# An encoder layer on one core: query transposes taken two heads at a time, the low parts of queries and keys later in VectorE's order, four weight casts later in the read-out

## The chip, the cores and the metric

The kernel runs on one core of a Trainium2 chip. The metric is the device time of one execution in microseconds (us). Before the change it is 1470.08 us, the median of three runs (1469.82 to 1471.71). The profile shows one further execution.

The engines are called by the profile's names: PE (TensorE matmul), PEld (its weight loads), DVE (VectorE), ACT (ScalarE), POOL (GpSimd) and SP, whose queue issues most DMAs.

## The reference, cut to what matters

One layer of a bidirectional encoder is applied to two sequences of 512 tokens with 1024 features. A state-space branch and a windowed attention branch are computed from the same normalized rows, gated, added, projected, and followed by a squared-ReLU MLP. The change touches the normalized queries and keys of the attention branch, and the place at which the key weights are prepared.

```
q, k, v, u, g_att, g_ssm = jnp.split(h @ w_in, IN_SPLITS, axis=-1)
q = rms_norm(q.reshape(bsz, seq_len, N_HEADS, HEAD_DIM), q_gain)     # 16 heads of 64
k = rms_norm(k.reshape(bsz, seq_len, N_KV_HEADS, HEAD_DIM), k_gain)  # 4 heads of 64
...
s = jnp.einsum('nqkgd,njkd->nkgqj', qb, kw) * scale + bias   # blocks of 128, three neighbours
s = jnp.where(mask[:, None, None], s, NEG_INF)
p = jax.nn.softmax(jnp.concatenate([s, sink_col], axis=-1), axis=-1)[..., :-1]
o = jnp.einsum('nkgqj,njkd->nqkgd', p, vw)
```

## The kernel before, in words

**Split numbers.** Products are made of float32 values split in a high part (rounded to fp32r, written by ACT) and a low part (the rest, written by DVE). A score product takes queries whose 128 rows hold the high part of 64 features in one half and the low part in the other, and keys that hold the same 64 features in both halves. So one product with the keys' high part `kh` and one with their low part `kl` give the whole score, whichever half of the queries is the high one.

**Read-out stage** (lines 890 to 950, about 326 to 414 us of the profile). A loop over 32 pairs of state groups, `q` in `range(NQ)`: the tables of pair q+5 are ordered on SP, `read_out(q)` multiplies on PE, `gelu(q)` takes the result out of PSUM on ACT. Beside it the stage works off a list of other products, and the table `casts` says behind which pair a quarter of the key weights `w_k` (and later of the value weights `w_v`) is loaded, cast to its high part by ACT, and given a low part by DVE. The staging tile of such a load (`c_raw`, `w_raw`) has two buffers. PE, ACT and DVE follow the written order here; SP's order is the scheduler's.

**Attention stage** (the function entered at line 1120, loop at 1199; about 451 to 685 us). A step is a pair (key head j, sequence sq), eight in all; a step has four units, one for each block of 128 queries (`qb` 0 to 3), and all of PE, ACT, DVE and POOL follow the written order. The document calls units by `qb`: a unit with qb 0 or 3 has scores 256 wide, one with qb 1 or 2 has 384. In each unit stand, interleaved:

- the scores and minima of the current unit (`cur.scores(h)`, `cur.largest(h)`, `cur.exp(h)` for four heads h). `largest` is one DVE instruction, L1052, that reads the score bank; there are two such banks, so `scores(2)` waits for `largest(0)`, and the next unit's `scores(0)` for `largest(2)`.
- the values of the unit before (`prev`): for each of its two or three key blocks i, four transposes on PE (`turn(i)`, L1064), a high part on ACT (`high(i)`, `ph`), a low part on DVE (`low(i)`, `pl`, L1073), and two products on PE (`value(i, 0)` with `ph`, `value(i, 1)` with `pl`, both L1080). `prev` has three blocks in the units qb 2 and 3, two in qb 0 and 1. Behind them ACT copies the lower half of the sums (`ol`, L1084), which DVE adds one unit later (`owed.add()`, L1090).
- a tile of the next step's queries: `project` on PE (L724), `square` on ACT and `power` on DVE and POOL, `norm` on DVE (L1012); then, one unit later and under the name `rows`, four transposes (`rows.turn()`, L1018), `rows.high()` on ACT (L1023) and `rows.low()` on DVE (L1027). Before the transposes POOL copies each head's 64 features a second time beside the first (L1013), so that a transpose of one head gives them in both halves.
- in a unit qb 0, the next step's keys: `key_copies` on POOL, `key_turn` (PE L981, ACT L982 for `kh`, DVE L983 for `kl`).
- in the units qb 1 and 2 of most steps, the low part of a piece of the next query weights (`lower`, `w_lo`, L719).

PSUM: scores have two banks, the transposes `tps` two, `acc` (projections and turned queries) three, and the sums `po` one.

Before the loop, `entry()` handles the first four query tiles and the values; tiles 0 to 2 are turned there, tile 3 in the loop's first unit.

Of the kernel before, what the change touches and what calls it, by code (L numbers as in the profile page):

```python
# [18 lines left out]
P = 128  # L19
# [44 lines left out]
def hybrid_layer(ctx, tc, x, xT, rel, onehot, early, w_qkv, w_ug, q_gain, k_gain, sink,  # L64
# [707 lines left out]
    with tc.tile_pool(name="ssmo", bufs=2, reuse_waits="tile") as sp:  # L772
# [129 lines left out]
        def last_cast():  # L902
            cast_owed.pop(0)()
            return dve_owed.pop()

        casts = {0: [last_cast], 1: [last_cast], 2: [lambda: w_k.piece(0)], 3: [lambda: w_k.piece(1)], 8: [lambda: w_k.piece(2)], 9: [lambda: w_k.piece(3)],
                 17: [lambda: w_v.piece(0)], 18: [lambda: w_v.piece(1)], 20: [lambda: w_v.piece(2)], 21: [lambda: w_v.piece(3)]}
# [45 lines left out]
    with tc.tile_pool(name="att", bufs=2, reuse_waits="tile") as ap:  # L953
# [21 lines left out]
        def key_turn(j, sq, kd):  # L975
            kh = ap.tile([P, HALF], F32R, tag="kh", name="kh")
            kl = ap.tile([P, HALF], F32R, tag="kl", name="kl")
            keys[j, sq] = (kh, kl)
            ps = tps()
            for t in range(4):  # L980
                PE.transpose(ps[:, t * P:(t + 1) * P], kd[:, t].rearrange("p a d -> p (a d)"), ident)  # L981
            S.activation(kh, ps, AF.Copy, scale=gain_k)  # L982
            V.scalar_tensor_tensor(kl, ps, gain_k, kh.bitcast(F32), op0=ALU.mult, op1=ALU.subtract)  # L983
            queries[j, sq] = ap.tile([P, G, HALF], F32R, tag="qa", name="qa")

        class Tile:
# [23 lines left out]
            def norm(self):  # L1010
                self.qn = ap.tile([P, G, 2, HD], F32, tag="qn", name="qn")
                V.tensor_mul(self.qn[:, :, 0], self.psv, self.rq[:, :, None].to_broadcast([P, G, HD]))  # L1012
                GP.tensor_copy(self.qn[:, :, 1], self.qn[:, :, 0])  # L1013

            def turn(self):
                self.pt = acc()
                for h in range(G):
                    PE.transpose(self.pt[:, h * P:(h + 1) * P], self.qn[:, h].rearrange("p a d -> p (a d)"), ident)  # L1018

            def high(self):  # L1020
                self.ptv = self.pt.rearrange("p (h t) -> p h t", h=G)
                self.dst = queries[self.key][:, :, self.t * P:(self.t + 1) * P]
                S.activation(self.dst, self.ptv, AF.Copy, scale=gain_q)  # L1023

            def low(self):
                dst = self.dst[64:128]
                V.scalar_tensor_tensor(dst, self.ptv[64:128], gain_q[64:128], dst.bitcast(F32),  # L1027
                                       op0=ALU.mult, op1=ALU.subtract)

# [100 lines left out]
        def entry():  # L1130
# [6 lines left out]
            for t in range(4):  # L1137
# [3 lines left out]
                if t == 0:  # L1141
                    key_turn(0, 0, kd)
                if old:
# [48 lines left out]
        pending = []  # L1192
        prev = owed = lower = None
        y_rows, made = [], None
# [4 lines left out]
        if True:  # L1199
            rows = entry()  # L1200
            for i, (j, sq) in enumerate(steps):
# [8 lines left out]
                for qb in range(NB):  # L1210
# [12 lines left out]
                    cur.scores(0)  # L1223
                    cur.largest(0)
                    if rows and not rows.qn:
                        rows.power()
# [3 lines left out]
                    if owed:  # L1230
                        owed.add()
                    cur.largest(1)
                    if n3:
                        prev.turn(0)
# [45 lines left out]
                    if kd:  # L1280
                        key_turn(*nxt, kd)
                    if div:
# [9 lines left out]
                    if rows:  # L1292
                        if not sooner:
                            rows.high()
                        rows.low()
                    project(4)
# [24 lines left out]
                if i == len(steps) - 2:  # L1321
                    hpool_cm.__exit__(None, None, None)
                    slot_a, slot_b = [opers.enter_context(tc.tile_pool(name=f"slot_{n}", bufs=1, side="right", reuse_waits="tile"))
                                      for n in "ab"]
                    y_tiles = [[[t_[:, 0:4, :], t_[:, 4:8, :]] for t_ in slot(slot_a)], split_slot()]
            ahead = Column(1)
            gs0 = wyp.tile([P, T, NSEQ, NCHUNK], F32, tag="y_lo", name="gs")
# [732 lines left out]
```

## Time and profile before

| | us |
|---|---|
| median of three runs | 1470.08 |
| profiled execution, its device time | 1469.22 |
| its span from first to last instruction | 1467.4 |
| entry and attention stage, about | 424 to 685 |
| read-out stage, about | 326 to 414 |

The profile page gives busy time and share of the span of each engine, the chain of work that ended last, and groups of instructions by line, engine and operation, with the idle time ahead of them and what ended it. The timeline lists instructions in order of time: start, duration, engine, line, operation, tiles written and read, and in brackets the idle time of that engine ahead of it with what released it. A row with x2 or x4 merges as many equal instructions. The profile's 1467.4 us lie 1.8 us below the execution's own time, and that lies 0.9 us below the median.

### The profile page before, as it was taken

How to read it: one execution, taken by the hardware profiler on the slowest of the kernel's cores; microseconds unless marked ns; L12 is line 12 of the kernel's file. 1: busy time of each engine (PE TensorE's matmuls, PEld its weight loads, DVE VectorE, ACT ScalarE, POOL GpSimd, SP SyncE). 2: the span in 40 equal slices, each digit the busy share in tenths (PEclk: the TensorE clock that was granted, in tenths of full speed). 3: DMA queues.
4: the chain of work that ended last, by engine and by line, in shares of the span. 5: the costliest groups of instructions: out<-in, count | busy, mean ns of one | idle time of the engine just before them, and what ended most of it. 6: DMA issues, size and time to landing. Idle time of an engine off the chain costs nothing.

```text
span 1467.4 us, 21580 instructions
## 1 busy us (share of the span) xinstructions
PE 1446.3 (99%) x7782; PEld 1234.1 (84%) x7782; DVE 1094.6 (75%) x1836; ACT 764.2 (52%) x1366; POOL 168.9 (12%) x270
## 2 busy tenths in 40 slices
PE   6999999999999999999999999999999999999998
PEld 5888888888999899987888888888888888888887
DVE  7799979975636889888974689877776588575653
ACT  5489862233426778787532355554554444333332
POOL 4111120000223333343101000000000000000000
PEclk9999999999999999999999999999999999999999
DMA  8355567259941413236964134544443894454441
GB/s 300 112 171 174 161 206 268 101 178 290 307 131 35 121 46 89 95 130 217 303 212 144 72 115 165 174 149 147 155 158 123 302 346 147 158 177 153 129 129 58
DMA packets 129239, 243.86 MB, mean 166 GB/s; under 512 B 16060, under 2 KB 59324, under 8 KB 129133
## 3 DMA queue, kind: packets, MB, share of 16 engines
q1 hardware_dynamic: 104684, 186.87, 40.4%
q10 hardware_dynamic: 21888, 46.15, 8.3%
q0 software_dynamic: 2560, 9.48, 2.0%
q8 instruction: 61, 1.00, 0.3%
q14 instruction: 46, 0.37, 0.1%
HBM read 173.20 MB, written 81.82 MB: 174 GB/s over the span
## 4 chain that ended last, share of the span: by engine, by line
PE 91%; DVE 3%; ACT 2%; DMA 1%; issue 1%; POOL 1%; SPq 0%; DVEq 0%; ACTq 0%; POOLq 0%
PE bank L115 14%; PE bank L116 14%; PE bank L117 14%; PE acc L141 11%; PE acc L724 8%; PE acc L753 5%; PE acc L115 3%; PE acc L117 3%; PE acc L116 3%; PE po L1080 2%; PE sps L604 2%; PE sps L1048 2%; PE sps L860 2%; PE tps L1064 2%; PE lag L619 1%
## 5 line engine op out<-in xcount | busy, mean ns | idle before, releaser
L116 PE MATMUL bank<-b_lo,a_hi 128*128 128x512 f32 x440 | 171.2, 389 | 0.0
L117 PE MATMUL bank<-b_hi,a_lo 128*128 128x512 f32 x440 | 171.2, 389 | 0.0
L115 PE MATMUL bank<-b_hi,a_hi 128*128 128x512 f32 x440 | 171.2, 389 | 0.0
L724 PE MATMUL acc<-w_hi,hT 128*128 128x256 f32 x768 | 165.0, 291 | 0.0
L141 PE MATMUL acc<-hT,c_hi 128*128 128x512 f32 x512 | 161.1, 394 | 0.0
L1933 ACT CAST a_hi<-d_a 128x1024 fp32r<-128x1024 f32 x55 | 58.0, 1054 | 178.1 <-PE bank L116 175.2
L1934 DVE TENSOR_TENSOR a_lo<-d_a,a_hi 128x1024 fp32r<-128x1024 f32 x55 | 67.3, 1223 | 99.4 <-ACT a_hi L1933 97.3
L724 PEld LDWEIGHTS acc<-w_hi,hT 128*128 128x128 f32 x768 | 126.7, 190 | 1.7
L141 PEld LDWEIGHTS acc<-hT,c_hi 128*128 128x128 f32 x512 | 94.6, 188 | 21.0 <-issue 2.5
L724 PE MATMUL acc<-w_lo,hT 128*128 128x256 f32 x384 | 108.2, 282 | 0.0
L141 PE MATMUL acc<-hT,c_lo 128*128 128x512 f32 x256 | 100.3, 392 | 0.0
L115 PE MATMUL bank<-act,u_hi 128*128 128x512 f32 x256 | 99.6, 389 | 0.0
L116 PE MATMUL bank<-act,u_hi 128*128 128x512 f32 x256 | 99.6, 389 | 0.0
L117 PE MATMUL bank<-act,u_lo 128*128 128x512 f32 x256 | 99.6, 389 | 0.0
L117 PEld LDWEIGHTS bank<-b_hi,a_lo 128*128 128x128 f32 x440 | 82.6, 188 | 17.3
L115 PEld LDWEIGHTS bank<-b_hi,a_hi 128*128 128x128 f32 x440 | 82.6, 188 | 17.1
L116 PEld LDWEIGHTS bank<-b_lo,a_hi 128*128 128x128 f32 x440 | 82.6, 188 | 17.1
L1058 ACT ACTIVATE p<-p,nmx 128x257 f32<-128x257 f32 (+1 forms) x128 | 72.1, 564 | 27.0 <-DVE nmx L1052 24.3
L724 PEld LDWEIGHTS acc<-w_lo,hT 128*128 128x128 f32 x384 | 73.0, 190 | 2.5
L1052 DVE CUSTOM_DVE_ANT_0 p<-sps,bias,nsink 128x256 f32<-128x256 f32 (+1 forms) x128 | 69.2, 541 | 2.9 <-PE sps L1048 0.4
L1717 ACT CAST u_hi<-s 128x512 fp32r<-128x512 f32 x64 | 39.3, 621 | 59.8 <-PE bank L116 43.1
L1934 DVE TENSOR_TENSOR b_lo<-k,b_hi 128x1024 fp32r<-128x1024 f32 x55 | 66.9, 1217 | 0.0
(387 smaller groups left out, 3622.9 us busy)
## 6 DMA issues: line engine op xcount, KB each, us to landing
d_a<-a_scr SPq DMA_DIRECT2D x55, 512.0 KB, 3.6
u_raw<-in_w_up_dram SPq DMA_DIRECT2D x32, 512.0 KB, 5.7
a_scr<-t ACTq DMA_DIRECT2D x64, 256.0 KB, 2.1
k<-in_w_down_dram SPq DMA_DIRECT2D x32, 512.0 KB, 5.7
a_scr<-a ACTq DMA_DIRECT2D x48, 256.0 KB, 3.3
c_raw<-in_w_ug_dram SPq DMA_DIRECT2D x44, 256.0 KB, 3.6
ct_scr<-ctab SPq DMA_DIRECT2D x16, 576.0 KB, 3.3
ctab_in<-ct_scr SPq DMA_DIRECT2D x32, 288.0 KB, 4.7
```

The costliest lines, as they stand in the source:

```text
L115: PE.matmul(ps, a[0], b[0], start=first, stop=False)
L116: PE.matmul(ps, a[0], b[1], start=False, stop=False)
L117: PE.matmul(ps, a[1], b[0], start=False, stop=last)
L141: PE.matmul(self.ps[s], self.w[p == 2][:, k, :], hT[s][p == 1][:, k, :], start=i % (3 * KT) == 0, stop=i % (3 * KT) == 3 * KT - 1)
L604: PE.matmul(ps[:, i * P:(i + 1) * P], bm[:, ri, g, :], u_sb[:, g, :], start=True, stop=True)
L724: PE.matmul(ps, act[p == 2][:, k, col:col + P], self.w[k // 4][p == 1][:, k % 4, :], start=i == 0, stop=i == 3 * KT - 1)
L753: PE.matmul(self.ps[s], w_g[self.m][p == 2][:, k, :], y_part(s, int(p == 1), k), start=k + p == 0, stop=k == KT - 1 and p == 2)
L1052: V.tensor_tensor_reduce(self.p[:, h, 1:1 + self.nk], self.s[h][:, 0:self.nk], biases[self.j][h][:, b0:b0 + self.nk], -1.0, nsink[:, hh:hh ...
L1058: S.activation(p, p, AF.Exp, bias=self.nmx[:, h:h + 1], scale=-1.0, accum_out=self.sums[:, h, self.qb:self.qb + 1])
L1717: S.copy(hi, src)
L1933: S.copy(hi, src)
L1934: V.tensor_sub(lo, src, hi.bitcast(F32))
```

## The change

Four things change.

1. **Queries.** `norm` writes each head once, without POOL's copy. `turn` transposes two heads at a time, so two transposes in place of four; the first head of a pair comes out in rows 0 to 63, the second in rows 64 to 127. `high` becomes two ACT instructions on 64 rows, one for the first heads and one for the second, each with 2x128 elements in a row in place of one with 4x128 on 128 rows; `low` becomes two DVE instructions of that shape, each writing the half of the rows that its input does not lie in.
2. **Place of the queries' low part.** In the loop it is held back (`low_rows`) and written in the next unit, behind `largest(1)`.
3. **Place of the keys' low part.** `key_turn` returns it; in the loop it is held back (`low_keys`) and written in the next unit (qb 1) behind `largest(0)`. In `entry()` it follows at once, as before.
4. **Casts of the key weights.** The quarters stand behind the pairs 4, 6, 9 and 11 in place of 2, 3, 8 and 9.

```diff
-        casts = {0: [last_cast], 1: [last_cast], 2: [lambda: w_k.piece(0)], 3: [lambda: w_k.piece(1)], 8: [lambda: w_k.piece(2)], 9: [lambda: w_k.piece(3)],
+        casts = {0: [last_cast], 1: [last_cast], 4: [lambda: w_k.piece(0)], 6: [lambda: w_k.piece(1)], 9: [lambda: w_k.piece(2)], 11: [lambda: w_k.piece(3)],
...
-            V.scalar_tensor_tensor(kl, ps, gain_k, kh.bitcast(F32), op0=ALU.mult, op1=ALU.subtract)
             queries[j, sq] = ap.tile([P, G, HALF], F32R, tag="qa", name="qa")
+            return lambda: V.scalar_tensor_tensor(kl, ps, gain_k, kh.bitcast(F32), op0=ALU.mult, op1=ALU.subtract)
...
             def norm(self):
-                self.qn = ap.tile([P, G, 2, HD], F32, tag="qn", name="qn")
-                V.tensor_mul(self.qn[:, :, 0], self.psv, self.rq[:, :, None].to_broadcast([P, G, HD]))
-                GP.tensor_copy(self.qn[:, :, 1], self.qn[:, :, 0])
+                self.qn = ap.tile([P, G, HD], F32, tag="qn", name="qn")
+                V.tensor_mul(self.qn, self.psv, self.rq[:, :, None].to_broadcast([P, G, HD]))
...
             def turn(self):
                 self.pt = acc()
-                for h in range(G):
-                    PE.transpose(self.pt[:, h * P:(h + 1) * P], self.qn[:, h].rearrange("p a d -> p (a d)"), ident)
+                for m in range(G // 2):
+                    PE.transpose(self.pt[:, m * P:(m + 1) * P], self.qn[:, 2 * m:2 * m + 2].rearrange("p a d -> p (a d)"), ident)
...
             def high(self):
-                self.ptv = self.pt.rearrange("p (h t) -> p h t", h=G)
-                self.dst = queries[self.key][:, :, self.t * P:(self.t + 1) * P]
-                S.activation(self.dst, self.ptv, AF.Copy, scale=gain_q)
+                q = queries[self.key][:, :, self.t * P:(self.t + 1) * P].rearrange("p (m e) t -> p m e t", e=2)
+                pt = self.pt[:, 0:G // 2 * P].rearrange("p (m t) -> p m t", m=G // 2)
+                self.halves = []
+                for e, (own, other) in enumerate(((slice(0, 64), slice(64, P)), (slice(64, P), slice(0, 64)))):
+                    hi, lo, src = q[own, :, e], q[other, :, e], pt[own]
+                    S.activation(hi, src, AF.Copy, scale=gain_q[own])
+                    self.halves.append((hi, lo, src, gain_q[own]))
...
             def low(self):
-                dst = self.dst[64:128]
-                V.scalar_tensor_tensor(dst, self.ptv[64:128], gain_q[64:128], dst.bitcast(F32),
-                                       op0=ALU.mult, op1=ALU.subtract)
+                for hi, lo, src, gain in self.halves:
+                    V.scalar_tensor_tensor(lo, src, gain, hi.bitcast(F32), op0=ALU.mult, op1=ALU.subtract)
...
                     cur.largest(0)
+                    if low_keys:
+                        low_keys()
+                        low_keys = None
...
                     cur.largest(1)
+                    if low_rows:
+                        low_rows()
+                        low_rows = None
...
                     if kd:
-                        key_turn(*nxt, kd)
+                        low_keys = key_turn(*nxt, kd)
...
                         if not sooner:
                             rows.high()
-                        rows.low()
+                        low_rows = rows.low
```

The lines of the changed kernel stand some three lines further down, so L1052 of before is L1055 there, L1027 is L1031, L1073 is L1076.

The first place is DVE's order around the start of a unit qb 1 (here of the second step). Before, from the keys' low part at the end of the unit qb 0 to the first `pl`:

```order
L983 SCALAR_TENSOR_TENSOR kl<-tps,gain_k,kh 128x512
L1027 SCALAR_TENSOR_TENSOR qa<-acc,gain_q,qa 64x4x128
L1052 ISA p,nmx<-sps,bias,nsink 128x384
L1052 ISA nmx 128x1
L1005 TENSOR_REDUCE ms<-sq 128x4
L1090 TENSOR_TENSOR ya<-po,ol 64x2x128 x2
L1052 ISA p,nmx<-sps,bias,nsink 128x384
L1052 ISA nmx 128x1
L1073 TENSOR_TENSOR pl<-tps,ph 128x512
```

The same place of the changed kernel, from the unit's first minimum to its first `pl`:

```order
L1055 ISA p,nmx<-sps,bias,nsink 128x384
L1055 ISA nmx 128x1
L984 SCALAR_TENSOR_TENSOR kl<-tps,gain_k,kh 128x512
L1005 TENSOR_REDUCE ms<-sq 128x4
L1093 TENSOR_TENSOR ya<-po,ol 64x2x128 x2
L1055 ISA p,nmx<-sps,bias,nsink 128x384
L1055 ISA nmx 128x1
L1031 SCALAR_TENSOR_TENSOR qa<-acc,gain_q,qa 64x2x128 x2
L1076 TENSOR_TENSOR pl<-tps,ph 128x512
```

Both low parts stood ahead of the first minimum; now both stand between the first minimum and the first `pl`. In the other units the queries' low part moves in the same way, and there is no `kl`.

The second place is ACT's order in the read-out, behind the last cast of the gates (`c_hi`). `ysb` is a pair's `gelu`, `st` the turning of a later pair's states. Before:

```order
L868 ACTIVATE ysb<-sps 128x256
L872 DMA y_scr<-ysb 128x512
L718 CAST w_hi<-w_raw 128x512
L868 ACTIVATE ysb<-sps 128x256
L845 COPY st<-h 64x512
L718 CAST w_hi<-w_raw 128x512
```

After:

```order
L868 ACTIVATE ysb<-sps 128x256
L872 DMA y_scr<-ysb 128x512
L868 ACTIVATE ysb<-sps 128x256
L845 COPY st<-h 64x512
L151 COPY sg<-acc 128x8x64
L868 ACTIVATE ysb<-sps 128x256
L872 DMA y_scr<-ysb 128x512
L718 CAST w_hi<-w_raw 128x512
```

The first cast stands two `gelu` later. On SP the load of its data keeps its place; the third and fourth loads of `w_raw` stand two sets of tables further back than before.

More of the change, by code (lines that the diff above doesn't have):

```diff
@@ L1141, in entry @@
                 if t == 0:
-                    key_turn(0, 0, kd)
+                    key_turn(0, 0, kd)()
                 if old:
@@ L1192, in hybrid_layer @@
         pending = []
-        prev = owed = lower = None
+        prev = owed = lower = low_rows = low_keys = None
         y_rows, made = [], None
@@ L1325, in hybrid_layer @@
                     y_tiles = [[[t_[:, 0:4, :], t_[:, 4:8, :]] for t_ in slot(slot_a)], split_slot()]
+            assert not low_rows and not low_keys
             ahead = Column(1)
```

## The prediction

> **What bounds the kernel now.** The page comes first: who is busy, and through whom the chain that ended last runs.
>
> ```profile
> PE 1446.3 (99%) x7782; PEld 1234.1 (84%) x7782; DVE 1094.6 (75%) x1836; ACT 764.2 (52%) x1366; POOL 168.9 (12%) x270
> ...
> PE 91%; DVE 3%; ACT 2%; DMA 1%; issue 1%; POOL 1%; SPq 0%; DVEq 0%; ACTq 0%; POOLq 0%
> ```
>
> PE carries the kernel, so a PE instruction less should shorten it. But the change lies in the attention stage, and there the second engine counts too. The windows of one step (one unit in a row, qb 0 to 3, each from its first score product to the next unit's):
>
> ```profile
> core 0: us, PE busy (x) PEld busy (x) DVE busy (x) ACT busy (x) POOL busy (x), PEclk, DMA share, GB/s
> 538.22:544.69 6.47, 6.47 (x53) 6.29 (x52) 4.98 (x16) 4.44 (x12) 2.36 (x5) 1.00 0.01 3
> 544.69:552.05 7.36, 7.32 (x51) 6.44 (x50) 6.93 (x19) 6.15 (x17) 1.80 (x4) 1.00 0.01 3
> 552.05:559.46 7.41, 7.41 (x57) 7.04 (x56) 6.83 (x17) 6.55 (x17) 1.84 (x4) 1.00 0.45 133
> 559.46:566.60 7.14, 7.14 (x56) 6.72 (x55) 6.17 (x17) 5.79 (x16) 4.16 (x6) 1.00 0.56 164
> ```
>
> The clock is full, PE has no slack, but DVE is at 92 to 94% in the middle units. So I ask when DVE's results are due. PE multiplies `pl` i in `value(i, 1)`, and stands still if `pl` is late. DVE's timeline of that step:
>
> ```profile
> 538.66 0.48 DVE L1052 CUSTOM_DVE_ANT_0 p<-sps,bias,nsink 128x256 f32<-128x256 f32 x1
> ...
> 540.68 0.69 DVE L1073 TENSOR_TENSOR pl<-tps,ph 128x512 fp32r<-128x512 f32 x1
> ...
> 544.45 0.75 DVE L983 SCALAR_TENSOR_TENSOR kl<-tps,gain_k,kh 128x512 fp32r<-128x512 f32 x1 [1.35 <-ACT kh L982]
> ...
> 546.31 0.62 DVE L1052 CUSTOM_DVE_ANT_0 p<-sps,bias,nsink 128x384 f32<-128x384 f32 x1
> ...
> 547.18 0.84 DVE L1090 TENSOR_TENSOR ya<-po,ol 64x256 f32<-64x256 f32 x2
> ...
> 548.60 0.69 DVE L1073 TENSOR_TENSOR pl<-tps,ph 128x512 fp32r<-128x512 f32 x1
> ...
> 550.14 0.68 DVE L719 TENSOR_TENSOR w_lo<-w_raw,w_hi 128x512 fp32r<-128x512 f32 x1
> 550.75 0.68 DVE L1073 TENSOR_TENSOR pl<-tps,ph 128x512 fp32r<-128x512 f32 x1
> ...
> 551.88 0.08 DVE L1052 DVE_READ_ACCUMULATOR2_ANT nmx<- 128x1 f32 x1
> 551.99 0.76 DVE L1027 SCALAR_TENSOR_TENSOR qa<-acc,gain_q,qa 64x512 fp32r<-64x512 f32 x1
> 552.78 0.62 DVE L1052 CUSTOM_DVE_ANT_0 p<-sps,bias,nsink 128x384 f32<-128x384 f32 x1
> ...
> 558.27 0.68 DVE L1073 TENSOR_TENSOR pl<-tps,ph 128x512 fp32r<-128x512 f32 x1
> ...
> 560.50 0.49 DVE L1052 CUSTOM_DVE_ANT_0 p<-sps,bias,nsink 128x256 f32<-128x256 f32 x1
> ...
> 562.52 0.69 DVE L1073 TENSOR_TENSOR pl<-tps,ph 128x512 fp32r<-128x512 f32 x1
> ```
>
> And PE's products that read these `pl`, with the transposes L1018 and a score product:
>
> ```profile
> 541.95 0.40 PE L1080 MATMUL po<-pl,va 128*128 128x512 f32 x1
> ...
> 544.88 0.34 PE L1048 MATMUL sps<-kl,qa 128*128 128x384 f32 x1
> ...
> 549.34 0.51 PE L1080 MATMUL po<-pl,va 128*128 128x512 f32 x1
> ...
> 551.50 0.47 PE L1080 MATMUL po<-pl,va 128*128 128x512 f32 x1
> ...
> 557.37 0.60 PE L1018 MATMUL acc<-ident,qn 128*128 128x128 f32 x4
> ...
> 559.22 0.39 PE L1080 MATMUL po<-pl,va 128*128 128x512 f32 x1
> ...
> 563.26 0.50 PE L1080 MATMUL po<-pl,va 128*128 128x512 f32 x1
> ```
>
> The reader is to see how close they are. `pl` ends at 548.60 + 0.69 = 549.29, PE starts 0.05 later: it waited. It waited at 563.26 too (562.52 + 0.69 + 0.05). At 551.50 the margin is 0.02, at 559.22 it is 0.22, at 541.95 it is 0.53. And DVE starts a unit late where the low parts stand ahead of it: its first minimum is 0.44 after the unit's start in qb 0, but 1.62 in qb 1, 0.73 in qb 2, 1.04 in qb 3.
>
> **The change part by part.**
>
> *Transposes.* L1018's group gives a mean of 277 ns, but four of them take 0.60, so they start (0.60 - 0.277)/3 = 0.108 us apart.
>
> ```profile
> L1018 PE MATMUL acc<-ident,qn 128*128 128x128 f32 x128 | 19.7, 277 | 1.2 <-POOL qn L1013 1.2
> ```
>
> Two fewer save 0.22 in each of 32 tiles, 6.9 us in all, but they stand behind `value(0, 1)`: a wait there is not shortened by them. The Trainium skill ("TensorE: Matmul & The Clock Gate", Part 4: PE-mode transpose) gives some 275 ns for such a transpose in a kernel's context; counted so, 64 of them would be 17.6 us. The row has that duration, but the starts are 0.108 apart, so the measurement decides for 6.9.
>
> *The low part, now a pair, in a new place.* One instruction of 64x256 of this kind is not in the trace. The additions L1090 have its shape: 0.42 each. The kind costs 0.07 more (0.76 against 0.69 at 512 elements), so 0.49, twice 0.98. Ahead of it the trace shows 0.11 (551.88 to 551.99) in place of an immediate start, behind it 0.03 (551.99 + 0.76 to 552.78). Together **1.12 us** between the second minimum and the first `pl`. Bounds: 0.79, if the pair took no longer than the single one with its gap, and 1.3. The Trainium skill ("VectorE: DVE Perf Modes", Two Vector instructions with no wait between them) says that an instruction whose start quadrant differs from the one before is held until that has finished; the pair changes halves each time, so all would be held. The gaps of 0.11 and 0.03 agree; without holding, the overlaps seen elsewhere would make it about 0.8, and the sum below 8 us smaller.
>
> *What moves earlier in return.* DVE no longer has the low part ahead of the first minimum, which then starts 0.04 after its scores (544.88 + 0.34): 0.57 into a 384-wide unit, 0.44 into a 256-wide one. But the additions behind it need ACT's `ol`, made at the start of a unit:
>
> ```profile
> 559.00 0.67 ACT L1023 ACTIVATE qa<-acc,gain_q 128x512 fp32r<-128x512 f32 x1
> 559.58 0.37 ACT L1001 ACTIVATE sq<-acc 128x256 f32<-128x256 f32 x1
> 559.97 0.58 ACT L1084 COPY ol<-po 64x512 f32<-64x512 f32 x1
> ```
>
> `ol` ends 1.09 into the unit. ACT's pair has sq's size, so 0.4 each, 0.8 for 0.58: `ol` comes 0.2 later (0.37 at most, with the 0.08 that the gain costs in the row above). So I credit qb 3 with 0.23 of its 0.60, qb 2 with nothing of its 0.16, and qb 1 with all 1.05, since `kl` gives `ol` time there.
>
> *By unit*, with every later DVE row of a unit moving along:
> - qb 0: `pl` ends 541.37 + 1.12 = 542.49, PE at 542.54 for 541.95: +0.59 - 0.22 = **+0.37**.
> - qb 1: -1.05 + 0.68 (`kl`, its 0.75 less 0.07 of overlap as behind `w_lo`) + 1.12 = 0.75. The second `pl` ends 551.43 + 0.75, PE at 552.23 for 551.50: **+0.73**; the saved transposes lie ahead of that wait.
> - qb 2: the third `pl` ends 558.95 + 1.12, PE at 560.12 for 559.22: **+0.90**.
> - qb 3: the first `pl` is 0.89 later, PE too: +0.89 - 0.22 = **+0.67**.
>
> A step grows by 2.67. Five steps (the second to fifth and the seventh) have this form: 13.4. The sixth has no `w_lo`, so its later `pl` aren't late and only the first is: 2.0 by the same working. In the eighth, without projections, I set nothing (between -1 and +1).
>
> *First step and entry.* Two waits go there: POOL's copy ahead of the transposes, and the first minimum behind `kl`.
>
> ```profile
> 455.60 0.66 PE L1018 MATMUL acc<-ident,qn 128*128 128x128 f32 x4 [0.82 <-POOL qn L1013]
> ...
> 460.11 0.44 PE L1048 MATMUL sps<-kh,qa 128*128 128x384 f32 x1 [0.47 <-DVE nmx L1052]
> ...
> L1013 POOL COPY qn<-qn 128x256 f32<-128x256 f32 x32 | 12.7, 398 | 29.7 <-DVE qn L1012 25.5 <-PE sps L1048 3.6 <-PE tps L1064 0.6
> ```
>
> The copy's 0.40 and 0.22 go in its unit qb 0; qb 1 comes out about even (-0.1), qb 2 and 3 grow by 0.9 and 0.7: +0.9. The entry saves three times 0.22, with PE always busy: -0.7. POOL's other copies lie beside PE's work: nothing.
>
> *Read-out.* ACT stood before the first key cast until its data had landed, and PE behind it, since `gelu` frees its banks:
>
> ```profile
> 336.10 0.62 ACT L718 CAST w_hi<-w_raw 128x512 fp32r<-128x512 f32 x1 [5.70 <-DMA w_raw<-in_w_qkv_dram]
> ...
> 337.06 0.49 PE L858 MATMUL sps<-u_sb,toep 128*128 128x128 f32 x2 [0.61 <-ACT ysb L868]
> 338.31 0.68 PE L860 MATMUL sps<-st,ctab_in 128*128 128x128 f32 x4 [0.77 <-ACT st L845]
> ```
>
> Two pairs later the data lies there, as its DMA keeps its place on SP. 0.61 + 0.77: **-1.4** (0 if another cast or a later load on SP takes over, -1.8 with PE's restarts).
>
> **Sum:** 13.4 + 2.0 + 0.9 - 0.7 - 1.4 = +14.2 on the profiled execution's 1469.2, which lies 0.9 below the median: **1483 us**, slower by 0.9%.
>
> **The rivals.**
>
> *PE keeps the bound.* DVE's busy time in the step is 24.9 of 28.4, four times 0.33 more would fit, and its waits for ACT's halves go:
>
> ```profile
> DVE qa L1027 <- ACT qa L1023: 10.5, 21, 0.8
> ...
> PEld po L1080 <- DVE pl L1073: 2.2, 8, 0.3
> ```
>
> Then 6.9 for the transposes, 1.4 in the read-out, these 2.2, and the first step's 0.4 and 0.5 go: 1469.2 - 11.4 = **1458**. It decides if `pl` still comes before PE asks, which in qb 1 needs both halves in under 0.4 us. The margins above speak against it: it is the place and not the total that counts. By the skill's 275 ns it would be 1447.
>
> *Even.* Each 0.1 less for the pair takes about 2.6 off (26 units). At 0.58 the gains elsewhere cancel the waits: **1469**. No row has two such instructions in that time.
>
> *The halves add their time and no more.* With the lower bound 0.79 the sum is 14.2 - 8.6 = 5.6: **1475**; that lies in the forecast's own case.
>
> **How the numbers follow.** The forecast's case, slower, has 0.72; PE keeping the bound 0.15; even 0.13. What a measurement of this kernel can tell from no change is about 0.2%, 3 us, so these are also the chances of slower, faster and same. The upper end takes 1.3 for the pair (+4.7): 1488. The lower goes past 0.79 for the pair to 1468, which covers the even case and leaves out the PE-bound one.
>
> **What would show it.** Right: in the units qb 0 to 3 PE waits in front of L1080 for `pl`, some 0.6 to 1.1 us a unit in place of 2.2 us over the stage; the units last about 6.8, 8.1, 8.3 and 7.8; the pair's instructions take 0.49; the wait at 337 is gone. Wrong: units shorter by 0.2 with no wait at L1080 (PE's bound), or instructions of the pair well under 0.4. DVE no longer waits for ACT's query halves in either case.

## The result, and the profile after

| | before | after |
|---|---|---|
| median of 4 runs each, us | 1469.95 (1469.59 to 1471.71) | 1488.34 (1487.40 to 1489.23) |
| ratio | | 1.0124, 95% interval 1.0109 to 1.0139 |
| profiled execution: span, us | 1467.4 | 1487.5 |

The change makes the kernel 1.2% slower, 18.4 us; the prediction said 13 (1483), and its range ended at 1488, just below the measured median. Direction and mechanism were right, the size was not.

The page of the changed kernel, busy engines and the chain that ended last:

```profile
PE 1445.8 (97%) x7718; PEld 1228.7 (83%) x7718; DVE 1104.8 (74%) x1868; ACT 774.7 (52%) x1398; POOL 154.6 (10%) x238
...
PE 80%; DVE 10%; ACT 4%; issue 3%; DMA 2%; POOL 1%; SPq 0%; DVEq 0%; ACTq 0%; POOLq 0%
```

PE is busy no longer than before, with 64 instructions less, and the span is 20 us longer: the difference is waiting. DVE, 3% of the chain before, now holds 10%. The view of waits over the attention stage says for what (engine and line, what it waited for and who made it; us in total, times, longest). First the kernel before, then the changed one, both from 451 to 700 us:

```profile
PEld po L1080 <- DVE pl L1073: 3.9, 12, 0.5
...
PE po L1080 <- DVE pl L1073: 0.4, 2, 0.2
```

```profile
PEld po L1083 <- DVE pl L1076: 34.4, 44, 1.4
...
PE po L1083 <- DVE pl L1076: 21.7, 35, 1.1
DVE ya L1093 <- ACT ol L1087: 2.8, 15, 0.2
```

The weight loads' wait for `pl`, 3.9 us before (2.2 in the prediction's row, which leaves out both ends of the stage), is now 34.4; that of the products, 0.4 before, is 21.7. The windows of the units qb 0 to 3 (qb 0 is the first row and belongs to the next step; columns as in the prediction):

```profile
573.27:580.25 6.98, 6.54 (x52) 6.15 (x50) 5.45 (x16) 4.86 (x13) 1.96 (x4) 1.00 0.07 23
548.70:556.82 8.12, 7.05 (x50) 6.20 (x49) 7.33 (x19) 6.65 (x19) 1.41 (x3) 1.00 0.01 3
556.82:565.35 8.53, 7.72 (x55) 6.74 (x54) 7.28 (x18) 6.54 (x17) 2.86 (x3) 1.00 0.40 114
565.35:573.27 7.92, 7.02 (x54) 6.51 (x52) 6.33 (x17) 6.20 (x17) 2.34 (x5) 1.00 0.58 158
sum 31.55, PE 28.32 PEld 25.60 DVE 26.39 ACT 24.26 POOL 8.57; mean PE 7.08 PEld 6.40 DVE 6.60 ACT 6.06 POOL 2.14
```

Units of 6.98, 8.12, 8.53 and 7.92 stand where 6.47, 7.36, 7.41 and 7.14 stood: a step is 3.2 longer, and no engine is full in it. The order of DVE in qb 2 shows why (timeline):

```profile
557.36 0.62 DVE L1055 CUSTOM_DVE_ANT_0 p<-sps,bias,nsink 128x384 f32<-128x384 f32 x1 [0.65 <-PE sps L1051]
...
558.51 0.84 DVE L1093 TENSOR_TENSOR ya<-po,ol 64x256 f32<-64x256 f32 x2 [0.19 <-ACT ol L1087]
559.38 0.62 DVE L1055 CUSTOM_DVE_ANT_0 p<-sps,bias,nsink 128x384 f32<-128x384 f32 x1
559.93 0.08 DVE L1055 DVE_READ_ACCUMULATOR2_ANT nmx<- 128x1 f32 x1
560.04 0.98 DVE L1031 SCALAR_TENSOR_TENSOR qa<-acc,gain_q,qa 64x256 fp32r<-64x256 f32 x2
561.05 0.69 DVE L1076 TENSOR_TENSOR pl<-tps,ph 128x512 fp32r<-128x512 f32 x1
...
564.26 0.69 DVE L1076 TENSOR_TENSOR pl<-tps,ph 128x512 fp32r<-128x512 f32 x1
```

The pair sits where the prediction put it: 0.11 behind the second minimum (559.93 to 560.04), 0.98 long, 0.03 ahead of `pl`. DVE waits at the unit's start, for scores and then for ACT's `ol`, and has the 1.12 us to do after that, so the first `pl`, and with it PE's product, comes later.

Where the 18 us lie, by the first score product of each step in the two profiled executions:

| | predicted | measured |
|---|---|---|
| up to the attention loop (read-out, entry) | -2.1 | -2.3 |
| first step | +0.9 | +1.3 |
| steps 2 to 5 and 7 | +13.4 | +14.0 |
| sixth step | +2.0 | +2.8 |
| eighth step, its first three units | 0 | +2.4 |
| sum | +14.2 | +18.2 |

The two spans differ by 1.9 more behind these units. The two profiled executions lie 1.6 further apart than the medians (after 0.9 above its own, before 0.7 below), so this may be scatter; no row was read for it. Single executions can differ by about 1 us in a row of this table too.

### The profile page after: what moved, and what is told of

It is laid out like the page before. It is cut to its first block, busy times and chain, and to the rows that moved or that the text cites. A ratio compares the mean times of both kernels' runs of the same rounds, so it can differ in the third digit from the quotient of the medians.

```text
span 1487.5 us, 21469 instructions
## 1 busy us (share of the span) xinstructions
PE 1445.8 (97%) x7718; PEld 1228.7 (83%) x7718; DVE 1104.8 (74%) x1868; ACT 774.7 (52%) x1398; POOL 154.6 (10%) x238
## 4 chain that ended last, share of the span: by engine, by line
PE 80%; DVE 10%; ACT 4%; issue 3%; DMA 2%; POOL 1%; SPq 0%; DVEq 0%; ACTq 0%; POOLq 0%
PE bank L115 13%; PE bank L116 13%; PE bank L117 13%; PE acc L141 11%; PE acc L724 5%; PE acc L115 3%; PE acc L117 3%; PE acc L116 3%; PE acc L753 3%; DVE p L1055 2%; PE sps L604 2%; PE sps L860 2%; DVE qa L1031 2%; DVE ya L1093 1%; DVE pl L1076 1%
## 5 line engine op out<-in xcount | busy, mean ns | idle before, releaser
L1055 DVE CUSTOM_DVE_ANT_0 p<-sps,bias,nsink 128x256 f32<-128x256 f32 (+1 forms) x128 | 69.3, 542 | 30.5 <-PE sps L1051 29.5
```

The source lines that it names most:

```text
L1055: V.tensor_tensor_reduce(self.p[:, h, 1:1 + self.nk], self.s[h][:, 0:self.nk], biases[self.j][h][:, b0:b0 + self.nk], -1.0, nsink[:, hh:hh ...
```

## The experiments

Times are medians. Unit and step lengths go from a unit's first score product to the next unit's in the profiled execution; a step is the fourth one.

| kernel | us | ratio to before, 95% interval | qb 0, 1, 2, 3 | step |
|---|---|---|---|---|
| before | 1469.95 | | 6.47, 7.36, 7.41, 7.14 | 28.4 |
| the change | 1488.34 | 1.0124 (1.0109 to 1.0139) | 6.97, 8.12, 8.53, 7.92 | 31.5 |
| e1 casts alone | 1468.12 | 0.999 (0.9981 to 1.0000) | 6.55, 7.35, 7.40, 7.14 | 28.4 |
| e2 pair, old places | 1476.05 | 1.0044 (1.0030 to 1.0058) | 6.49, 7.83, 7.52, 7.51 | 29.4 |
| e3 places alone | 1483.30 | 1.0098 (1.0083 to 1.0113) | 7.20, 7.86, 8.17, 7.52 | 30.8 |
| e5 half more | 1516.67 | 1.0320 (1.0304 to 1.0335) | 7.49, 8.62, 9.06, 8.46 | 33.6 |
| e6 keys alone | 1473.35 | 1.0026 (1.0017 to 1.0036) | 6.55, 8.02, 7.40, 7.14 | 29.1 |
| e7 low pair a unit later | 1470.20 | 1.0004 (0.9995 to 1.0014) | 6.26, 6.96, 7.52, 6.79 | 27.5 |
| e8 ACT's pair first | 1462.89 | 0.9954 (0.9939 to 0.9969) | 6.26, 6.98, 7.53, 6.72 | 27.5 |
| e9 single, ACT first | 1462.09 | 0.9947 (0.9932 to 0.9962) | 6.46, 6.61, 7.41, 6.95 | 27.4 |
| e10 eighth step late | 1486.97 | 1.0122 (1.0105 to 1.0138) | 6.97, 8.11, 8.54, 7.91 | 31.5 |
| e11 banks rotated | 1473.02 | 1.0027 (1.0016 to 1.0038) | 6.27, 6.96, 7.52, 6.80 | 27.6 |
| e12 weights to qb 3 and 0 | 1459.63 | 0.9932 (0.9919 to 0.9944) | 6.25, 6.58, 7.54, 6.83 | 27.2 |
| e13 the same, single | 1462.38 | 0.9951 (0.9938 to 0.9965) | 6.75, 6.61, 7.41, 6.95 | 27.7 |

**The change taken apart: casts, pair, places.** e1 is the kernel before with one line changed:

```diff
-        casts = {0: [last_cast], 1: [last_cast], 2: [lambda: w_k.piece(0)], 3: [lambda: w_k.piece(1)], 8: [lambda: w_k.piece(2)], 9: [lambda: w_k.piece(3)],
+        casts = {0: [last_cast], 1: [last_cast], 4: [lambda: w_k.piece(0)], 6: [lambda: w_k.piece(1)], 9: [lambda: w_k.piece(2)], 11: [lambda: w_k.piece(3)],
```

> The kernel before with only the four key casts moved (they come at iterations 4, 6, 9 and 11 of the read-out). Theory (the casts take away two waits of PE at 337 and 338 us, 0.61 + 0.77, and nothing else): the attention loop starts about 1.4 us earlier than the 451.36 of before, and the time is 1.4 us lower, 1468.5. Rival (a later load or another cast takes over the wait): the loop starts at 451.4 as before, 1470.

The median is 1.2 lower (interval 0 to 2.8). The attention loop starts at 450.2 to 451.4 in the three unpaired kernels with the old casts (before, e3, e6) and at 448.5 to 449.3 in those with the moved ones (e1, e9, e13), 1.9 apart in the mean for the 1.4 of the forecast. The term is there, by the place of the loop more than by the median, whose interval reaches no change; single executions scatter by 1.

e2 keeps the pair and undoes the places and the casts.

```diff
-                        low_keys = key_turn(*nxt, kd)
+                        key_turn(*nxt, kd)()
...
-                        low_rows = rows.low
+                        rows.low()
```

> The changed kernel's paired transposes and its two ACT and two DVE instructions, but both low parts in the places of before (right behind the ACT pair, and kl right behind kh), and the casts as before. Theory (the place of the low part costs the time, not the pair): the low parts start about 0.26 later than before, since ACT's pair takes 0.93 for 0.67, and last 0.22 longer, so the first minimum of a unit is some 0.5 later, and with the margins before value(i, 1) a step grows by qb 0 -0.2, qb 1 +0.5, qb 2 +0.4, qb 3 +0.3, together 1.0, a third of the 3.16 measured; over 6.5 steps +6, less about 1.3 at the entry and in the first step: 1475 (1470 to 1479). Rival (the pair's extra work on DVE and ACT costs the time wherever it stands): steps of 31.5 as in the changed kernel, about 1489. Second rival (PE's bound shows as soon as the place is undone): steps of 27.5, 1462.

1476.05, and steps 1.0 longer than before in place of 3.2, as the theory said. About two thirds of the loss go with the place.

e3 is the opposite: the single low part of before, in the new places (cut here to the queries; `kl` moves as in e6).

```diff
+                    if low_rows:
+                        low_rows()
+                        low_rows = None
                     if n3:
                         prev.turn(0)
...
-                        rows.low()
+                        low_rows = rows.low
```

> The kernel before, with its four transposes, its copy on POOL, its single low part and its casts, but with both low parts in the places of the changed kernel. Theory (the place costs the time): 0.76 and the gaps of 0.11 and 0.03 stand ahead of the first pl, 0.90 for the pair's 1.12; a step grows by qb 0 +0.5, qb 1 +0.5, qb 2 +0.8, qb 3 +0.7, together 2.5, times 6.5, and something in the eighth step: 1485 (1482 to 1489). Rival (the pair is what costs): no wait at value(i, 1) beyond those of before, 1470.

1483.30: the place alone makes a ratio of 1.0098 of the change's 1.0124, without any pair. The rival (the pair itself) would have left 1470.

**A dose.** e5 runs the first half of the low pair a second time.

```diff
-                for hi, lo, src, gain in self.halves:
+                for hi, lo, src, gain in self.halves + self.halves[:1]:
```

> The changed kernel with a third instruction in each low pair, which computes the first half once more (same values). Theory (what stands ahead of the first pl sets the unit): 0.49 more ahead of every first pl, and 0.49 more in every unit that waits for pl, 26 units and two in the eighth step: a step of about 33.5 for 31.55, 1488 + 13 = 1501 (1499 to 1503). Rival (PE's waits come from ACT's longer pair or from the doubled number of instructions only in part): less than half of that, under 1495.

The step is 33.6, as expected (33.5), each unit 0.5 longer. The time, 1516.67, misses its forecast by 15.7 us, since the added delay also met other waits. One unit, qb 3 of the second step, holds 9.4 of them (17.84 for the 8.46 of the fourth step), and the eighth step is 3.5 longer than in the changed kernel (26.4 for 22.9) where 1.0 was expected; the rest was not taken apart. The waits of that execution from 505 to 524:

```profile
POOL ya L1122 <- DMA fac<-rs_scr: 16.3, 1, 16.3
ACT p L1061 <- POOL p L1043: 10.5, 1, 10.5
DVE qn L1012 <- POOL rq L1008: 8.8, 1, 8.8
PEld acc L1017 <- DVE qn L1012: 8.1, 1, 8.1
PE acc L1017 <- DVE qn L1012: 7.9, 1, 7.9
```

POOL stood in its queue for a DMA, and behind it the small POOL operations on which ACT and DVE wait. A dose is read from the units that it touches, not from the total. For the opposite, the pair without its second instruction (e4), there is no time, so the dose goes one way only.

**The keys' low part.** e6 moves `kl` alone, in the kernel before.

```diff
                     cur.largest(0)
+                    if low_keys:
+                        low_keys()
+                        low_keys = None
```

> The kernel before with only the keys' low part kl moved behind the next unit's first minimum; the query low part stays in its place, single. Theory: in the place of before kl lies in the time in which DVE waits for ACT's query half (1.35 us of waiting ahead of kl, the half ends at 545.49), so its move frees nothing and adds 0.68 ahead of the first pl of qb 1, where PE waits already: +0.68 in each of 7 units, +4.5: 1474 (1473 to 1475). Rival (kl ahead of the first minimum is what holds unit qb 1 up, so the move pays or is even): 1467 to 1470.

Unit qb 1 goes from 7.36 to 8.02, +0.66, and the time up by 0.26%, 3.8 us. In its old place `kl` cost nothing that its move could save: DVE waited there for ACT anyway (1.35 ahead of `kl` in the prediction's rows).

**Where the pair would cost nothing.** e7 puts the low pair at the end of the unit, ahead of the next ACT pair; e8 puts both low parts back and ACT's pair right behind its transposes (in qb 0 the low pair goes with it, ahead of `kl`).

```diff
e7:
-                    if low_rows:
-                        low_rows()
-                        low_rows = None
                     if n3:
                         prev.turn(0)
...
+                    if low_rows:
+                        low_rows()
+                        low_rows = None
                     if rows:
                         if not sooner:
                             rows.high()
e8 (beside e2, with the moved casts):
                     if rows:
                         rows.turn()
+                    early = rows and kd
+                    if early:
+                        rows.high()
+                        rows.low()
...
-                    sooner = rows and n3 == 2 and not kd
+                    sooner = rows and not early
...
                     if rows:
-                        if not sooner:
-                            rows.high()
-                        low_rows = rows.low
+                        if not early:
+                            rows.low()
```

> The changed kernel with the query low pair moved on by most of a unit: from behind the second minimum to the end of that unit, behind the last pl and ahead of the next ACT pair. Theory (the pair costs nothing where DVE is idle): DVE waits 0.65 to 1.5 us for the next unit's scores there, and the ACT pair is long done, so the pair needs no wait, and every first pl comes 1.1 earlier; the units fall to PE's bound, about 6.25, 7.1, 7.2, 6.8, together 27.4 for the 28.4 of before: -1.0 times 6.5, -2.3 at the entry and in the read-out, about -1 in the first step: 1460 (1457 to 1463). Rival (DVE's total of 26.4 in a step, with its gaps, is the limit wherever the pair stands): a step of 29 or more, over 1472.

> The changed kernel with both low parts in the places of before, and with ACT's query pair right behind its transposes, ahead of the fourth exponential (in qb 0 also ahead of kh). Theory (in the old places the low pair waits for ACT's late pair, 0.6 to 1.0 us a unit): the pair then starts when DVE comes free, the first minimum comes 0.5 to 1.0 earlier than with the old places alone; units of about 6.3, 7.2, 7.3, 7.0, a step of 27.8: 1462 (1459 to 1466). Rival (the delayed exponential takes over the wait, or DVE's total does): no better than the old places alone, 1474 to 1476 less the 2 of the casts.

Both steps are 27.5 (27.4 and 27.8 were expected), 4 us less than the change's: with the pair where DVE has time, the products' waits for `pl` fall from 21.7 to 0.8 us in e7 and 0.5 in e8. e8 is 0.46% faster than before. e7's forecast of 1460 failed: its gain was lost elsewhere. Behind the attention stage PE stood still for 4.7 us, and the granted clock was 0.50 from 863.8 to 870.7 us. The waits of e7 and then of e11 there:

```profile
PE bank L115 <- ACT u L1703: 4.7, 1, 4.7
```

```profile
PE bank L115 <- DVE a L1714: 7.4, 1, 7.4
```

PE's first product of the next stage (`bank`) waits until ACT has copied `u` from an `acc` tile; the orders of all engines behind the attention stage are those of the changed kernel, which has no such wait. What differs is the order in which the `acc` banks came free in the attention stage, and so which of the three the later tiles got. e11 tried to undo it, with the eighth step's low pair in the changed kernel's place (beside e7):

```diff
                     cur.largest(1)
+                    if low_rows and i == len(steps) - 1:
+                        low_rows()
+                        low_rows = None
```

> The run with the low pair a unit later, but in the eighth step with the pair behind the second minimum as in the changed kernel, which only changes which PSUM bank comes free when, and so which of three banks the later accumulators lie in. Theory (that run lost 4.9 us at 859 and some 3.5 us of half clock behind it because its first product of the next stage lay in the bank that ACT still had to copy from): the wait is gone, and the time is about 1470.2 - 8 = 1462 (1460 to 1465). Rival (the wait has another cause, or the steps' gain is lost elsewhere): 1469 or more.

That failed: the wait became one for DVE's read of another `acc` tile, 7.4 us, and the time 1473. The places of the tiles in the programs built from these kernels fit the reuse of a bank. The first `bank` tile lies in PSUM bank 0 in each of them. In the kernel before, the changed one, e8 and e10, which have no such wait, the last tile in that bank was the third-last `acc`; in e7 it was the last but one, which ACT copies to `u`, and in e11 the last, which DVE reads for `a`. e10 has e7's eighth step and no wait, e11 the changed kernel's and a longer one: the low pair's place in the eighth step alone does not decide it. No run here took the wait out of e7, so what e7 would reach without it is not shown.

**Is it the pairing that gains in e8?** e9 is the kernel before with the moved casts and the lines of e8's diff, so it has four transposes and the single low part.

> The kernel before (four transposes, POOL's copy, one single low part in its old place) with the moved casts and with ACT's query half right behind its transposes, as in the run with ACT's pair first. Theory (PE sets the steps once no pl is late, and the pairing saves its two transposes, 0.22 a unit, and POOL's copy in the first step): steps of 27.5 + 0.9 = 28.4, as before, less 1.2 for the casts: 1468 (1466 to 1470), some 5 to 6 above the run with ACT's pair first. Rival (all the gain of that run comes from ACT's order, and two transposes fewer save nothing): 1463.

The rival won: 1462.09, as fast as e8. Their windows of qb 1 and 2, e8 and then e9, tell why:

```profile
539.41:546.39 6.98, 6.84 (x49) 6.13 (x48) 6.85 (x20) 6.24 (x18) 1.41 (x3) 1.00 0.01 4
546.39:553.92 7.53, 7.48 (x55) 6.81 (x53) 7.40 (x19) 7.13 (x18) 1.68 (x3) 1.00 0.50 126
```

```profile
540.97:547.58 6.61, 6.61 (x52) 6.36 (x50) 6.45 (x19) 5.81 (x16) 1.80 (x4) 1.00 0.02 5
547.58:554.99 7.41, 7.41 (x57) 7.02 (x56) 7.30 (x18) 6.86 (x18) 2.04 (x4) 1.00 0.50 133
```

In e8 DVE is busy 6.85 of 6.98 and 7.40 of 7.53: it looks like the bound there, and PE's two saved transposes don't show. In e9 PE has no gap. My expectation took before's qb 1 of 7.36 for PE's own time, and 0.75 of it was waiting, though its row says busy for 7.32: short waits hardly show as idle time. e12 takes the weights' `w_lo` out of these two units, in e8; e13 does it in e9:

```diff
-                    if extra:
+                    if extra and (qb > 1 or i in (0, len(steps) - 2)):
                         lower = extra.pop(0)()
```

> The run with ACT's pair first (paired transposes, low parts in their old places, casts moved), and in the second to fifth step the weight pieces are asked for at the ends of qb 2 and 3, so that their w_hi and w_lo fall into qb 3 and the next qb 0 instead of qb 1 and 2. Theory (with ACT's pair first DVE is full in qb 1 and 2, 6.86 of 6.98 and 7.40 of 7.52, and that hides the pairing's saving; qb 3 and 0 have room, 6.11 of 6.73 and 5.45 of 6.28): units with pieces of about 6.3, 6.4, 7.2, 6.9, a step of 26.8 for 27.5: 4 us less in the steps, 1459 (1457 to 1461). Rival (DVE's total in the step is the limit, wherever w_lo lies, or the later pieces make the projections wait): 1462 to 1464.

> The same move of the weight pieces in the run with the single low part and ACT's half first. Theory: its steps (6.46, 6.61, 7.41, 6.95) show no wait for pl, so PE sets them and the move brings nothing but what the second step's wait for a piece (9.37 in its qb 2) changes: 1462 (1460 to 1463). If this gains as much as the paired kernel, the gain is not the pairing's.

1459.63 and 1462.38, close to both forecasts, and e12 is 0.68% faster than before. But the step of e12 is 27.2 and not the 26.8 of its theory, so the total was met in part by luck. Of the 4.2 us by which its steps together are shorter than e8's, 3.6 lie in the second and third, where e8 had units of 9.28, 7.62 and 8.38, in part behind DMAs (ACT waited 2.1 there for `w_raw`); the fourth and the fifth are 0.3 shorter each. The 2.7 us between e12 and e13 are 0.2%, about what a measurement can tell, and the move cost the single kernel 0.28 in qb 0 (6.47 in e9, 6.75 in e13). Against e9 the paired kernel gains 2.5. So it is somewhat faster once DVE has room, but 0.22 a unit is not shown. The windows of e12:

```profile
531.05:537.30 6.25, 6.25 (x51) 6.07 (x50) 6.02 (x18) 5.70 (x15) 1.97 (x4) 1.00 0.11 34
537.30:543.88 6.58, 6.58 (x50) 6.07 (x48) 6.20 (x18) 5.35 (x16) 1.42 (x3) 1.00 0.07 25
543.88:551.41 7.53, 7.53 (x54) 6.76 (x53) 6.81 (x18) 6.63 (x17) 2.96 (x3) 1.00 0.24 72
551.41:558.25 6.84, 6.84 (x54) 6.41 (x53) 6.72 (x19) 6.55 (x18) 2.27 (x5) 1.00 0.61 174
```

PE is busy throughout by this view. Against e9 only qb 0 shows the whole 0.22 (6.25 for 6.46) and qb 3 half of it. qb 1 bears out that DVE was the bound in e8 (6.98 to 6.58); qb 2 stays at 7.53 although DVE went from 7.40 to 6.81, so there it was not DVE's total. Short waits are left in qb 2, as the timeline shows:

```profile
544.24 0.98 DVE L1031 SCALAR_TENSOR_TENSOR qa<-acc,gain_q,qa 64x256 fp32r<-64x256 f32 x2 [0.64 <-ACT qa L1026]
...
547.53 0.68 DVE L1076 TENSOR_TENSOR pl<-tps,ph 128x512 fp32r<-128x512 f32 x1
...
548.27 0.50 PE L1083 MATMUL po<-pl,va 128*128 128x512 f32 x1
```

DVE waits for ACT's pair, the first `pl` ends at 548.21, and PE's product starts right behind it and holds PE for 0.34 (0.23 in e9).

**The eighth step.** e10 is the changed kernel with the pair at the unit's end in the eighth step's qb 0 alone.

```diff
-                    if low_rows:
+                    if low_rows and i < len(steps) - 1:
                         low_rows()
                         low_rows = None
...
+                    if low_rows:
+                        low_rows()
+                        low_rows = None
                     if rows:
                         if not sooner:
                             rows.high()
```

> The changed kernel, with the query low pair moved to the unit's end in the eighth step alone (one unit, qb 0; it stays behind the second minimum everywhere else). Theory (the eighth step's 2.4 come from the pair ahead of its first pl, and from the half clock that PE's two waits bring there): the first pl starts behind ph at 670.14 for 670.83, PE's wait there is 0.7 shorter, the granted clock stays at 1.00 (0.50 from 672 to 675 in the changed kernel), and unit qb 0 of the eighth step lasts about 6.7 for 8.29: 1.2 to 2 us less than the changed kernel, 1486.5. Rival (ACT's casts of y or the DMA of y set that unit): the unit stays over 7.8, 1488.

The theory is half right. The clock stays at 1.00, and PE gets its first `pl` product 0.70 earlier in the unit (3.62 for 4.32), as the theory said; but the unit is 8.00 long. The waits of e10 there:

```profile
PE acc L1180 <- DVE qa L1031: 1.3, 1, 1.3
PE po L1083 <- ACT ph L1071: 1.0, 1, 1.0
```

The late pair holds its `acc` tile, and `first_column` needs the bank for its second accumulator. The unit stays over the rival's 7.8, but not by the rival's ACT or DMA: the new place has a deadline of its own. The eighth step's first three units are 1.1 shorter than in the changed kernel (21.8 for 22.9); the ratios to before, 1.0122 and 1.0124, do not tell the two kernels apart.

## Why the mechanism was right, and which terms of the sum were wrong

The time missed the range, by a little: 1488.34 for 1483 (1468 to 1488). The step that failed most is a term of the sum: "In the eighth, without projections, I set nothing". It measured 2.4 us, the largest of the errors. The others are the sixth step (2.8 for 2.0), the five steps of one form (14.0 for 13.4) and the first step (1.3 for 0.9). The range could not take this up: its upper end was worked out from a longer pair alone, and the +1 that the prediction allowed for the eighth step was not added to it.

**The pair and its place: right.** 0.11 ahead, twice 0.49, 0.03 behind: 1.12 as predicted. The Trainium skill ("VectorE: DVE Perf Modes", Two Vector instructions with no wait between them) holds such an instruction until the one before has finished; the trace agrees, with the 0.11, 0.98 and 0.03 above, and e5's third instruction added its full length too (1.50 for 0.98). e3 shows that the place costs even without the pair, e7 and e8 that the pair costs little in another place.

**The units: the first `pl` right, two small terms missed.** In qb 0 `pl` starts 3.58 after the unit's start for 2.46 before: 1.12 later. Yet the unit grew by 0.50 and not by 0.37. PE's rows of the changed kernel:

```profile
577.60 0.50 PE L1083 MATMUL po<-pl,va 128*128 128x512 f32 x1 [0.44 <-DVE pl L1076]
577.94 0.40 PE L724 MATMUL acc<-w_hi,hT 128*128 128x256 f32 x2
```

The product that waited holds PE for 0.34 to the next start; before, without a wait, the next came at 542.18 behind 541.95, 0.23. So a new wait costs some 0.11 of restart. The prediction knew of restarts in the read-out and left them out of "qb 0" and "qb 2", which had none before. The second term is ACT: its pair takes 0.93 (group below) where the prediction took 0.8, so `ol` and the additions came later still (the 0.19 at 558.51), 0.1 in qb 2 and qb 3.

```profile
L1031 DVE SCALAR_TENSOR_TENSOR qa<-acc,gain_q,qa 64x256 fp32r<-64x256 f32 x58 | 28.0, 483 | 1.4
L1026 ACT ACTIVATE qa<-acc,gain_q 64x256 fp32r<-64x256 f32 x58 | 26.9, 464 | 0.4
```

Together a step of the predicted form grew by 3.16 and not by 2.67. In the sum this shows little, by luck: the kernel's second step, the first of the five, grew by 1.4 only, as part of it was waiting for a DMA before (its qb 2 lasted 8.38, and ACT waited 1.3 in it for `w_raw`).

**"The sixth has no `w_lo`, so its later `pl` aren't late and only the first is: 2.0": mis-sized, 2.8.** The credit failed in qb 2 (7.41 to 8.53). DVE in that unit, which starts at 619.47:

```profile
620.97 0.42 DVE L1005 TENSOR_REDUCE ms<-sq 128x4 f32<-128x256 f32 x1 [0.31 <-ACT sq L1001]
621.57 0.85 DVE L1093 TENSOR_TENSOR ya<-po,ol 64x256 f32<-64x256 f32 x2 [0.19 <-ACT ol L1087]
...
624.12 0.69 DVE L1076 TENSOR_TENSOR pl<-tps,ph 128x512 fp32r<-128x512 f32 x1
```

The first `pl` starts 4.65 into the unit, before 2.96 (611.69 in a unit that starts at 608.73): 1.69 later and not 1.12. Waiting for ACT's `sq` and `ol`, which stand behind the longer pair, makes up the difference.

**"In the eighth, without projections, I set nothing": the largest error, 2.4.** The windows of its first unit in the changed kernel:

```profile
669.00:670.00 1.00, 0.17 (x2) 0.00 (x0) 0.94 (x4) 0.98 (x3) 1.00 (x2) 1.00 0.81 287
670.00:671.00 1.00, 0.73 (x3) 0.48 (x3) 0.95 (x3) 1.00 (x6) 1.00 (x1) 1.00 1.11 373
671.00:672.00 1.00, 0.43 (x1) 0.39 (x2) 1.00 (x3) 1.00 (x4) 0.20 (x1) 0.77 0.81 225
672.00:673.00 1.00, 1.00 (x4) 0.84 (x4) 1.00 (x4) 1.00 (x5) 0.34 (x1) 0.50 0.95 385
...
674.00:675.00 1.00, 1.00 (x4) 0.81 (x3) 0.55 (x1) 0.56 (x2) 0.59 (x1) 0.52 0.15 53
675.00:676.00 1.00, 1.00 (x6) 0.87 (x6) 0.00 (x0) 0.21 (x1) 0.00 (x0) 1.00 0.04 16
```

Without projections PE has nothing to fill a wait. It stood for ACT's `ph` (0.96) and for `pl` (0.70), and got its first `pl` product 4.32 into the unit for 3.21 before: 1.1 later. The granted clock was 0.50 from 671.54 to 674.95, and the products of `first_column` started some 0.43 apart for 0.23. The unit grew by 1.7 (8.29 for 6.58), the next by 0.7. e3, with the low parts in the same places, shows the same clock from 668 to 671; e2 and e8, with the old places, keep 1.00 and have units of 6.71 and 6.41 there.

How much of it is the clock? e11 has the changed kernel's place in this step, and the same two waits, but kept 1.00:

```profile
645.58 0.50 PE L1083 MATMUL po<-ph,va 128*128 128x512 f32 x1 [0.95 <-ACT ph L1071]
...
647.03 0.49 PE L1083 MATMUL po<-pl,va 128*128 128x512 f32 x1 [0.71 <-DVE pl L1076]
```

Its unit lasts 7.17. So of the 1.7, about 0.6 come with the waits and 1.1 with the half clock. The next unit's 0.7 hangs on neither: that unit, 7.09 in the changed kernel, lasts 7.10 in e11 and 7.11 and 7.43 in e2 and e8. Nor does the half clock explain the median: one of the four runs of the changed kernel has a mean granted clock of 1.00 and took 1488.44. An edit's cost is not to be set to zero where its cover is thinnest.

**The rest.** The first step was 0.4 worse. The read-out and the entry were as predicted, and the two waits of PE at 337 and 338 us are gone: the view of waits from 326 to 345 us shows none of PE. The rival "PE keeps the bound" fell with the waits for `pl`, "even" with the pair's 0.49. That PE had no slack, as the prediction read from its busy time, was not so, though: the kernel before had waits in qb 1 that ACT's order alone takes away (e9: 7.36 to 6.61), with no pairing.

## What to carry to other kernels

Moving work "behind the first wait" is only free if the engine is idle there: look for where it waits for input (here 0.65 to 1.5 us at a unit's end) and put the work just ahead of that, with its own input made early. A saving on the engine that carries the kernel shows only if no other engine becomes the bound in the units concerned; count busy time by unit and not by stage, and check by start times too, as short waits hardly show as idle time. Where the filler work is missing, as in a last step, a new wait can bring the half clock with it and cost more than its length (here 1.7 for 1.1; 0.6 where the clock stayed full).

## What was not expected of the hardware

- The granted TensorE clock fell to 0.50 behind 3.4 us in which PE was busy for about half, and stayed there from 671.54 to 674.95, 3.4 us. The Trainium skill ("TensorE: Matmul & The Clock Gate", Part 1: The HAM clock gate) speaks of one idle window of about 3.4 us; the length agrees, but here PE was not idle. PE's activity in these microseconds alone does not decide it: e11, as little busy at the same place, kept 1.00, and so did the kernel before, busy 0.44, 1.00 and 0.64 in three us there. The windows ahead of the fall in the changed kernel, and of the same products in e11:

```profile
668.12:671.54 3.42, 1.78 (x11) 1.19 (x9) 3.30 (x11) 3.37 (x10) 2.52 (x3) 1.00 0.90 271
```

```profile
643.70:647.10 3.40, 1.73 (x11) 1.25 (x10) 3.27 (x9) 3.35 (x10) 2.52 (x3) 1.00 1.02 412
```

- A PE product of 512 columns that had to wait for `pl` held PE 0.11 us longer than one that had not (0.34 for 0.23; right behind a transpose it is 0.31 to 0.32 without a wait).
- Not the chip's doing but the program's: moving one pair of DVE instructions changed which PSUM bank the last accumulators got, and with it came waits of 4.7 and 7.4 us some 200 us further on (e7, e11), with the same order of instructions there.
